# A two-layer decoder trunk on one core: the last K tile pair of the second two w2 blocks by seven products, and four sums of the first two blocks kept in PSUM

## The chip, the cores and the metric

The kernel runs on one core of a Trainium2 chip. Its time is the device time of one execution in microseconds (us); the median of several runs counts. The engines of the core work side by side and meet through semaphores: TensorE (PE in the profile; its weight loads are PEld) multiplies, VectorE (DVE) and ScalarE (ACT) do elementwise work, GpSimd (POOL) hardly anything here, and SyncE (SP) issues the DMA loads. TensorE writes its products into PSUM, which has eight banks of 128 x 512 float32.

## The reference, cut to what matters

Two layers over 256 tokens of width 2048: a short gated convolution mixer, then latent attention, each followed by the same MLP with 8192 hidden units. The change is in the MLP:

```
def sq_relu_mlp(x, w1, w2):
    return jnp.square(jax.nn.relu(x @ w1)) @ w2

h = layer_norm(ALPHA * h + mix, ln_g[layer, 0], ln_b[layer, 0])
h = layer_norm(ALPHA * h + sq_relu_mlp(h, mlp_w1[layer], mlp_w2[layer]),
               ln_g[layer, 1], ln_b[layer, 1])
```

x has 256 rows, w1 is 2048 x 8192, w2 is 8192 x 2048, all float32.

## The kernel before

**Split numbers.** Each float32 operand is kept as two parts: `hi`, the value rounded to fp32r, and `lo`, the rest. A product takes three matmuls, hi·hi, hi·lo and lo·hi (`dot`, L283 to L285). For weights the two parts are made on the core: a raw half unit of 128 x 1024 is loaded by SP (L132), ScalarE casts it to `hi` (L121), VectorE subtracts to get `lo` (L122). There are five raw buffers and eight pairs of `hi` and `lo`. `take` hands the next weights to TensorE and prepares further ones, as far as five half units ahead; a buffer's next load waits until its last reader is done.

**The MLP** (`mlp`, run as MLP 1 and MLP 3) goes through the 8192 hidden units in 8 passes of 1024, q = 0 to 7. A pass has a w1 stage, 8 products with w1 that give 8 hidden tiles (128 units x 256 tokens, collected by `hidden`), and a w2 stage, which multiplies these 8 tiles (the K tiles) with the pass's rows of w2 and adds to the accumulator `acc`: 2 token halves t by 4 column blocks n of 512.

**Plain blocks** (`down`): for each K tile and token half one `dot` of 128 x 512, so 8 x 2 x 3 = 48 matmuls per block; then `put` adds the block's two PSUM sums to `acc` on VectorE (L578).

**Seven products.** In the passes q = 1 to 6 (`FAST`) blocks 0 and 1 are done in another way (`first_pair`, `fast_products`): a pair of K tiles, two token halves and two column blocks make a 2 x 2 by 2 x 2 block product, and that is formed from seven products of sums instead of eight plain ones (`FACTORS` lists their names and factors). The sums of hidden tiles, S1 to S4, are made in `form` during the w1 stage. The sums of weights, T1 to T4, are made in `prepare` from two raw half units: beside three casts and three subtractions of 1024 columns, VectorE does L154 (1024 columns), L157, L160 and the low half of T4 (512 columns each). Such a unit counts as three in the look-ahead. Each of the seven products has a PSUM bank of its own and is summed there over the four K tile pairs of the pass. Then `keep` adds the seven sums to `acc` or to `sums` in SBUF (L588), seven additions per pass; those named "1", "5", "7" and "6" (`OWN`) go to `sums`. In the last pass `fold` (L607) adds `sums` into `acc` in six operations, beside the w1 stage.

**Banks.** `mlp` runs with all eight banks. The w1 stage turns between banks 0 and 1, the seven products use 2, 3, 4, 5, 6, 7 and 0 (`KEPT`), block 2 uses 1 and 2, block 3 uses 3 and 4. In the passes 1 to 4 of MLP 3 `extra` is `turn_residual`: four transposes for each token half into bank 5 or 6, and one addition on VectorE (L946).

**What sets the order.** Each engine runs its instructions in one fixed order. That order is made when the kernel is built: a scheduler places the instructions by priority and by its own estimate of when things become ready, so VectorE's queue interleaves the splitting of later weights with the collecting of sums. An instruction that waits holds up everything behind it on its engine.

One fast pass is therefore: w1 stage (256 matmuls, 512 and 256 columns in turn), four seven-product units (84 matmuls), block 2 and block 3 (96 matmuls).

Of the kernel before, what the change touches and what calls it, by code (L numbers as in the profile page):

```python
# [10 lines left out]
F32 = mybir.dt.float32  # L11
# [5 lines left out]
P = 128  # L17
# [17 lines left out]
NB = 4  # L35
BW = D // NB
FAST = range(1, NQ - 1)
FIRST = (0, 1, 2, 4, 6, 8, 12, 16)
HEAD = 4
GROUP = 3  # L40
# [10 lines left out]
def trunk(ctx: ExitStack, tc: tile.TileContext, xT, vecs, w_first, w_in, w_out, w_kv, w_q, w_uk, w_uv,  # L51
# [18 lines left out]
    def halves(w):  # L70

        lead = len(w.shape) - 2
        return [(w,)] if lead == 0 else [h for i in range(w.shape[0]) for h in halves(w[i])]
# [6 lines left out]
    def mlp_stream(l):  # L80
        out = []
        for q in range(NQ):
            out += halves(w1[l, q * QC:(q + 1) * QC])
            plain = halves(w2[l, q, 2:] if q in FAST else w2[l, q])
            fast = [(w2f[l, q, j, 0], w2f[l, q, j, 1]) for j in range(QC // 2)] if q in FAST else []
            at = 0 if q or q not in FAST else len(plain) // 2
            out += plain[:at] + fast + plain[at:]
        return out

    stream += mlp_stream(0) + halves(w_kv) + halves(w_q)  # L90
# [94 lines left out]
    def psum(name, bank=None):  # L185

        bank = Banks.next() if bank is None else bank
        return (pmm if bank < 4 else Banks.more).tile([P, 512], F32, tag=f"mm{bank}", name=name)
# [89 lines left out]
            yield ps  # L278


    def dot(ps, w, x, first, last):

        nc.tensor.matmul(ps, x[0], w[0], start=first, stop=False)  # L283
        nc.tensor.matmul(ps, x[0], w[1], start=False, stop=False)  # L284
        nc.tensor.matmul(ps, x[1], w[0], start=False, stop=last)  # L285

    def held(x, t):

        return [x[:, o + t * P:o + (t + 1) * P] for o in (0, T)]

    def wide_rows(w, kk):

        return [v[:, 4 * kk:4 * kk + 4, :].rearrange("p a c -> p (a c)") for v in w]

    def down(x, put, n, banks=(None, None), amid=None):

        ps = [psum("ps_d", bank) for bank in banks]
        for j in range(len(x) // 2):
            w, = take(1)
            for kk in range(2):  # L300
                k = 2 * j + kk
                for t in range(2):
                    dot(ps[t], wide_rows(w, kk), held(x[k], t), k == 0, k == len(x) - 1)
            if amid and 2 * j + 2 == len(x) // 2:
                amid()
        for t in range(2):
            put(n, t, ps[t])
# [10 lines left out]
                    dot(ps, wide_rows(ws[n, k // 2], k % 2), held(x[k], t), k == 0, k == len(x) - 1)  # L318
                put(n, t, ps)

    OWN, KEPT = ("1", "5", "7", "6"), (2, 3, 4, 5, 6, 7, 0)


    FACTORS = (("3", "S4", "22"), ("1", "11", "11"), ("5", "S1", "T1"), ("7", "S3", "T3"),
               ("2", "12", "21"), ("6", "S2", "T2"), ("4", "22", "T4"))

    def fast_products(ps, x, forms, j, n):

        b, = take(1)
        a = {"11": held(x[2 * j], 0), "12": held(x[2 * j + 1], 0), "22": held(x[2 * j + 1], 1)}  # L330
        for i in range(4):
            a[f"S{i + 1}"] = [forms[:, j, o, i * P:(i + 1) * P] for o in range(2)]
        for p, l, r in FACTORS:
            dot(ps[p], b[r], a[l], j == 0, j == n - 1)

    def whole(ps, out):

# [216 lines left out]
    def mlp(idx, ln, blocks, fast, begin=None, extra=None):  # L554
# [14 lines left out]
        def block(n, t):  # L569
            return acc[:, t, n * BW:(n + 1) * BW]  # L570
# [7 lines left out]
                nc.vector.tensor_tensor(block(n, t), block(n, t), ps, ALU.add)  # L578

        sums = fast.tile([P, 4, BW], F32, name=f"sums{idx}")  # L580

        def keep(p, ps):

            at = sums[:, OWN.index(p)] if p in OWN else block(*{"2": (0, 0), "3": (1, 0), "4": (0, 1)}[p])
            if q == 0 or q == FAST[0] and p in OWN:
                nc.scalar.copy(at, ps)
            else:
                nc.vector.tensor_tensor(at, at, ps, ALU.add)  # L588

        def first_pair(h, forms, banks):  # L590

            n = QC // 2
            ps = {p: psum(f"ps_f{p}", bank) for (p, _, _), bank in zip(FACTORS, banks)}
            for j in range(n):
                fast_products(ps, h, forms, j, n)
            for p in ps:
                keep(p, ps[p])

        def fold():

            s1, s5, s7, s6 = (sums[:, i] for i in range(4))
            both = acc[:, 1, :2 * BW].rearrange("p (b c) -> p b c", b=2)
            right = acc[:, :, BW:2 * BW]
            two = lambda v: v.unsqueeze(1).to_broadcast([P, 2, BW])
            for d, a, b in ((block(0, 0), block(0, 0), s1), (s6, s6, s1), (block(1, 0), block(1, 0), s6),
                            (s7, s7, s6), (both, both, two(s7)), (right, right, two(s5))):
                nc.vector.tensor_tensor(d, a, b, ALU.add)  # L607
                yield

        for q in range(NQ):  # L610
            ht = act.tile([P, QC, 2 * T], F32R, tag="c", name=f"h{idx}_{q}")
            h = [ht[:, k, :] for k in range(QC)]
            forms = None
            if q in FAST:
                forms = act.tile([P, QC // 2, 2, 4 * P], F32R, tag="a2", name=f"forms{idx}_{q}")
            pair = []

            def pair_tile(m):

                if m % 2 == 0:  # L620
                    pool = (act, "ab") if m % 4 else (fast, "fp")
                    t = pool[0].tile([P, 2 * T], F32, tag=pool[1], name="fp")
                    pair.append(t.rearrange("p (i t) -> p i t", i=2))
                return pair[-1]

            def form(j):
                (a11, a21), (a12, a22) = ((pair[j][:, i, :P], pair[j][:, i, P:]) for i in range(2))
                sf = fast.tile([P, 4, P], F32, tag="sf", name="sf")
                s1, s2, s3, s4 = (sf[:, i, :] for i in range(4))
                nc.vector.tensor_tensor(s1, a21, a22, ALU.add)  # L630
                nc.vector.tensor_tensor(s3, a21, a11, ALU.subtract)
                nc.vector.tensor_tensor(s2, s1, a11, ALU.subtract)
                nc.vector.tensor_tensor(s4, a12, s2, ALU.subtract)
                split(forms[:, j, 0, :], forms[:, j, 1, :], sf.rearrange("p i c -> p (i c)"))

            def hidden(m, ps, evac, *func):
                both = pair_tile(m) if q in FAST else None
                f = both[:, m % 2, :] if both is not None else tmp.tile([P, T], F32, tag="fh", name="fh", bufs=3)
                evac(ps, f, *func)
                if not func:  # L640
                    nc.scalar.activation(f, f, AF.Relu)  # L641
                nc.scalar.activation(f, f, AF.Square)
                if both is None:
                    put_split(h[m], f)
                elif m % 2:
                    at = ht[:, m - 1:m + 1, :]
                    split(at[:, :, :T], at[:, :, T:], both)
                    form(m // 2)

            if q == 0:  # L650
                for m in range(QC):
                    if m < GROUP:
                        if m == 0:
                            ws = ln.ws if ln.ws else group_of(GROUP)
                            if not ln.ws:
                                mm_wide(ws, ln.xd)
                            ln.finish()
                        ps = ws[m][1]
                    else:
                        ws = [(take(), psum("ps_w"))]  # L660
                        mm_wide(ws, ln.xd)
                        ps = ws[0][1]
                    hidden(m, ps, ln.weighted, AF.Relu)
                    if m > 0:
                        normal()
                if begin:
                    begin(range(1))
                acc = act.tile([P, 2, D], F32, tag="a1", name=f"acc{idx}")
            else:
                folds = fold()  # L670
                for m, ps in enumerate(products(QC, xhl, TURNED, (0, 1))):
                    hidden(m, ps, whole)
                    if q == NQ - 1:
                        next(folds, None)
                        if begin:
                            begin(range(max(2 * m, 1), 2 * m + 2))

            if q == NQ - 1:
                blocks(block, put, h)
                return  # L680
            if q == 0:
                for n in range(NB):
                    down(h, put, n)
            else:
                first_pair(h, forms, KEPT)
                for n, banks in ((2, (1, 2)), (3, (3, 4))):
                    down(h, put, n, banks)
                    if extra and n == 2 and q <= NB:
                        for t in range(2):
                            extra(block, q - 1, t, 5 + t)  # L690

    def to_wide(block, put, h):

# [406 lines left out]
```

## Time and profile before

| | us |
|---|---|
| median of 3 runs | 2025.86 (2025.52 to 2026.03) |
| the profiled execution | 2028.49 |
| its span, first to last instruction | 2026.4 |
| VectorE, low half of a raw half unit (L122), 710 times | 1.222 each |
| ScalarE, cast of a raw half unit (L121), 710 times | 1.051 each |
| VectorE, addition of a plain block's sum (L578), 64 times | 0.681 each |
| VectorE, additions of seven-product sums (L588), 76 times | 0.681 each |
| w loads of 512 KB (`in_w_dram`), 416 times, issue to landing | 4.3, the median |
| w2f loads of 512 KB (`in_w2f_dram`), 96 times | 3.6, the median |

The durations of one instruction contain a tail that overlaps the next one on the same engine, so that a row of them advances faster than the sum of durations. Records of matmuls overlap as well; the distance between two starts is what a matmul costs.

### The profile page before, as it was taken

How to read it: one execution, taken by the hardware profiler on the slowest of the kernel's cores; microseconds unless marked ns; L12 is line 12 of the kernel's file. 1: busy time of each engine (PE TensorE's matmuls, PEld its weight loads, DVE VectorE, ACT ScalarE, POOL GpSimd, SP SyncE). 2: the span in 40 equal slices, each digit the busy share in tenths (PEclk: the TensorE clock that was granted, in tenths of full speed). 3: DMA queues.
4: the chain of work that ended last, by engine and by line, in shares of the span. 5: the costliest groups of instructions: out<-in, count | busy, mean ns of one | idle time of the engine just before them, and what ended most of it. 6: DMA issues, size and time to landing. Idle time of an engine off the chain costs nothing.

```text
span 2026.4 us, 30052 instructions
## 1 busy us (share of the span) xinstructions
PE 2018.3 (100%) x11240; PEld 1763.1 (87%) x11240; DVE 1605.8 (79%) x2467; ACT 1176.2 (58%) x1797; POOL 2.3 (0%) x21
## 2 busy tenths in 40 slices
PE   9999999999999999999999999999999999999998
PEld 8888888988888888888889998898888888888886
DVE  7667667787787978979678978776879798797966
ACT  6444445576565665656556655566656566565651
POOL 0000000000000000000000000000000000000000
PEclk9999999999999999999999999999999999999999
DMA  8666666564746657475654543656475664746663
GB/s 298 204 188 189 190 187 186 177 196 146 249 148 226 204 170 239 143 240 194 220 179 146 179 134 126 197 177 196 137 249 167 198 227 142 248 160 210 220 201 120
DMA packets 106849, 385.30 MB, mean 190 GB/s; under 512 B 11856, under 2 KB 12752, under 8 KB 106448
## 3 DMA queue, kind: packets, MB, share of 16 engines
q1 hardware_dynamic: 106560, 383.27, 59.3%
q8 instruction: 88, 1.44, 0.3%
q14 instruction: 57, 0.47, 0.1%
q10 hardware_dynamic: 144, 0.13, 0.0%
HBM read 381.25 MB, written 2.10 MB: 189 GB/s over the span
## 4 chain that ended last, share of the span: by engine, by line
PE 99%; DMA 0%; DVE 0%; SPq 0%; issue 0%; ACT 0%; DVEq 0%
PE ps_u L199 20%; PE ps_l L199 13%; PE ps_u L203 11%; PE ps_d L285 7%; PE ps_d L283 7%; PE ps_d L284 7%; PE ps_l L203 7%; PE ps_f L284 4%; PE ps_f L285 4%; PE ps_f L283 4%; PE ps_w L233 2%; PE ps_w L231 2%; PE ps_w L232 2%; PE ps_g L231 1%; PE ps_g L233 1%; PE ps_g L232 1%
## 5 line engine op out<-in xcount | busy, mean ns | idle before, releaser
L122 DVE TENSOR_TENSOR lo<-raw,hi 128x1024 fp32r<-128x1024 f32 x710 | 859.8, 1222 | 314.1 <-ACT hi L121 243.0
L121 ACT CAST hi<-raw 128x1024 fp32r<-128x1024 f32 x710 | 742.4, 1051 | 460.0 <-PE ps_u L199 108.0
L199 PE MATMUL ps_u<-xhl,hi 128*128 128x512 f32 x1792 | 621.0, 391 | 0.0
L203 PE MATMUL ps_u<-xhl,lo 128*128 128x256 f32 x1792 | 499.5, 280 | 0.0
L199 PEld LDWEIGHTS ps_u<-xhl,hi 128*128 128x128 f32 x1792 | 334.2, 187 | 72.4
L203 PEld LDWEIGHTS ps_u<-xhl,lo 128*128 128x128 f32 x1792 | 338.6, 189 | 1.8
L283 PE MATMUL ps_d<-hi,h 128*128 128x512 f32 x640 | 249.8, 390 | 0.0
L285 PE MATMUL ps_d<-hi,h 128*128 128x512 f32 x640 | 249.1, 389 | 0.0
L284 PE MATMUL ps_d<-lo,h 128*128 128x512 f32 x640 | 249.0, 389 | 0.0
L199 PE MATMUL ps_l<-xhl_a,hi 128*128 128x512 f32 x704 | 243.5, 392 | 0.0
L203 PE MATMUL ps_l<-xhl_a,lo 128*128 128x256 f32 x704 | 194.8, 279 | 0.0
L199 PEld LDWEIGHTS ps_l<-xhl_a,hi 128*128 128x128 f32 x704 | 131.7, 187 | 29.5
L283 PEld LDWEIGHTS ps_d<-hi,h 128*128 128x128 f32 x640 | 120.2, 188 | 25.0 <-DVE fh L340 0.3
L285 PEld LDWEIGHTS ps_d<-hi,h 128*128 128x128 f32 x640 | 120.1, 188 | 24.9
L284 PEld LDWEIGHTS ps_d<-lo,h 128*128 128x128 f32 x640 | 120.2, 188 | 24.7
L203 PEld LDWEIGHTS ps_l<-xhl_a,lo 128*128 128x128 f32 x704 | 132.2, 188 | 0.2
L199 PE MATMUL ps_l<-z,hi 128*128 128x512 f32 x240 | 83.9, 398 | 0.0
L641 ACT ACTIVATE fp<-fp 128x256 f32<-128x256 f32 x96 | 40.0, 416 | 72.6 <-DVE fp L340 71.9
L121 ACT CAST hi_t<-raw_t 128x1024 fp32r<-128x1024 f32 x48 | 50.4, 1050 | 42.9 <-DVE raw_t L154 33.4
L233 PE MATMUL ps_w<-xd,hi 128*128 128x258 f32 x256 | 73.0, 285 | 0.0
L231 PE MATMUL ps_w<-xd,hi 128*128 128x258 f32 x256 | 72.6, 284 | 0.0
L232 PE MATMUL ps_w<-xd,lo 128*128 128x258 f32 x256 | 72.4, 283 | 0.0
(257 smaller groups left out, 3134.5 us busy)
## 6 DMA issues: line engine op xcount, KB each, us to landing
raw<-in_w_dram SPq DMA_DIRECT2D x416, 512.0 KB, 4.3
raw<-in_w2f_dram SPq DMA_DIRECT2D x96, 512.0 KB, 3.6
raw<-in_w_in_dram SPq DMA_DIRECT2D x88, 512.0 KB, 3.6
raw<-in_w_out_dram SPq DMA_DIRECT2D x32, 512.0 KB, 3.9
raw<-in_w_o_dram SPq DMA_DIRECT2D x32, 512.0 KB, 4.3
raw<-in_w_kv_dram SPq DMA_DIRECT2D x10, 512.0 KB, 4.2
raw<-in_w_q_dram SPq DMA_DIRECT2D x8, 512.0 KB, 4.5
raw<-in_w_uk_dram SPq DMA_DIRECT2D x8, 512.0 KB, 4.4
```

The costliest lines, as they stand in the source:

```text
L121: nc.scalar.copy(hi, src)
L122: nc.vector.tensor_tensor(lo, src, hi.bitcast(F32), ALU.subtract)
L199: nc.tensor.matmul(ps, w[blk // 8][0][:, blk % 8, :], x, start=first, stop=False)
L203: nc.tensor.matmul(ps[:, :T], w[blk // 8][1][:, blk % 8, :], x[:, :T], start=False, stop=last)
L231: nc.tensor.matmul(ps[:, :W], hi, x[k][:, :W], start=k == 0, stop=False)
L232: nc.tensor.matmul(ps[:, :W], lo, x[k][:, :W], start=False, stop=False)
L233: nc.tensor.matmul(ps[:, :W], hi, x[k][:, W:], start=False, stop=k == NC - 1)
L283: nc.tensor.matmul(ps, x[0], w[0], start=first, stop=False)
L284: nc.tensor.matmul(ps, x[0], w[1], start=False, stop=False)
L285: nc.tensor.matmul(ps, x[1], w[0], start=False, stop=last)
L641: nc.scalar.activation(f, f, AF.Relu)
```

## The change

In the fast passes, blocks 2 and 3 are no longer plain over all eight K tiles. Block 3 and then block 2 are done plainly over the first six, and the last pair of K tiles (`SECOND`) goes through seven products for both blocks together. These seven are not summed in PSUM: each is finished on its own and collected at once, into `acc` or into `sums`. They go round the banks c, b, d, a, c, b, d.

The four sums "1", "5", "7" and "6" of blocks 0 and 1 now stay in banks 4 to 7 from the first fast pass to the last, summed over all six passes, and `fold` reads them there. Only the sums "3", "2" and "4" of these blocks are collected in each pass. `sums` in SBUF now holds the four of blocks 2 and 3, and `fold` has twelve operations and a copy, two operations per hidden tile. All else in the MLP's fast passes has the four banks 0 to 3, in roles a, b, c, d that change from pass to pass (`turn`). One matmul of a plain block, the middle one of the first `dot` of block 2, is done as two of 256 columns. The residual's transposes come after the first pair of K tiles of block 3 and of block 2, one token half each. The host lays out w2 for both pairs of blocks.

```diff
@@ mlp_stream
-            plain = halves(w2[l, q, 2:] if q in FAST else w2[l, q])
-            fast = [(w2f[l, q, j, 0], w2f[l, q, j, 1]) for j in range(QC // 2)] if q in FAST else []
-            at = 0 if q or q not in FAST else len(plain) // 2
-            out += plain[:at] + fast + plain[at:]
+            if q not in FAST:
+                out += halves(w2[l, q])
+                continue
+            out += [(w2f[l, q, 0, j, 0], w2f[l, q, 0, j, 1]) for j in range(QC // 2)]
+            for n in (3, 2):
+                out += halves(w2[l, q, n, :SECOND])
+            out.append((w2f[l, q, 1, SECOND, 0], w2f[l, q, 1, SECOND, 1]))
@@ dot
-    def dot(ps, w, x, first, last):
+    def dot(ps, w, x, first, last, two=False):
...
-        nc.tensor.matmul(ps, x[0], w[1], start=False, stop=False)
+        for at in (slice(0, T), slice(T, 2 * T)) if two else (slice(None),):
+            nc.tensor.matmul(ps[:, at], x[0], w[1][:, at], start=False, stop=False)
@@ down
-            if amid and 2 * j + 2 == len(x) // 2:
+            if amid and j == 0:
@@ mlp
+        own = {}
+
+        def gather(at, ps, first=False):
+            if first:
                 nc.scalar.copy(at, ps)
             else:
                 nc.vector.tensor_tensor(at, at, ps, ALU.add)
 
+        def alone(p, g):
+
+            return block(*{"2": (2 * g, 0), "3": (2 * g + 1, 0), "4": (2 * g, 1)}[p])
+
         def first_pair(h, forms, banks):
 
             n = QC // 2
-            ps = {p: psum(f"ps_f{p}", bank) for (p, _, _), bank in zip(FACTORS, banks)}
+            ps = {p: psum(f"ps_f{p}", bank) for p, bank in zip("324", banks)}
+            if q == FAST[0]:
+                own.update({p: psum(f"ps_o{p}", 4 + i) for i, p in enumerate(OWN)})
             for j in range(n):
-                fast_products(ps, h, forms, j, n)
-            for p in ps:
-                keep(p, ps[p])
+                def put_product(p, w, x):
+                    if p in OWN:
+                        dot(own[p], w, x, q == FAST[0] and j == 0, q == FAST[-1] and j == n - 1)
+                    else:
+                        dot(ps[p], w, x, j == 0, j == n - 1)
+
+                fast_products(h, forms, j, put_product)
+            for p in "324":
+                gather(alone(p, 0), ps[p])
+
+        def second_pair(h, forms, banks):
+
+            c, b, d, a = banks
+            for n, two, free, split_at in ((3, (b, c), a, None), (2, (d, a), b, (0, 0))):
+                def amid():
+                    if extra and q <= NB:
+                        extra(block, q - 1, 3 - n, free)
+
+                down(h[:2 * SECOND], put, n, two, amid, split_at)
+            places = iter((c, b, d, a, c, b, d))
+
+            def put_product(p, w, x):
+                ps = psum(f"ps_s{p}", next(places))
+                dot(ps, w, x, True, True)
+                if p in OWN:
+                    gather(sums[:, OWN.index(p)], ps, q == FAST[0])
+                else:
+                    gather(alone(p, 1), ps)
+
+            fast_products(h, forms, SECOND, put_product)
 
         def fold():
...
+            t = raws.tile([P, 1024], F32, tag="raw", name=f"fold{idx}")
+            nc.scalar.copy(t[:, :BW], own["1"])
+            for g in range(2):
+                s1, s5, s7, s6 = (own[p] if g == 0 else sums[:, i] for i, p in enumerate(OWN))
...
+        turn = 0, 1, 2, 3
...
-                first_pair(h, forms, KEPT)
-                for n, banks in ((2, (1, 2)), (3, (3, 4))):
-                    down(h, put, n, banks)
-                    if extra and n == 2 and q <= NB:
-                        for t in range(2):
-                            extra(block, q - 1, t, 5 + t)
+                a, b, c, d = turn
+                first_pair(h, forms, (c, d, a))
+                second_pair(h, forms, (c, b, d, a))
+                turn = a, c, b, d
```

More of the change, by code (lines that the diff above doesn't have):

```diff
@@ L37 @@
 FAST = range(1, NQ - 1)
+SECOND = QC // 2 - 1
 FIRST = (0, 1, 2, 4, 6, 8, 12, 16)
@@ L293, in wide_rows, with down @@
         return [v[:, 4 * kk:4 * kk + 4, :].rearrange("p a c -> p (a c)") for v in w]
-    def down(x, put, n, banks=(None, None), amid=None):
+    def down(x, put, n, banks=(None, None), amid=None, two=None):
         ps = [psum("ps_d", bank) for bank in banks]
@@ L302, in down @@
                 for t in range(2):
-                    dot(ps[t], wide_rows(w, kk), held(x[k], t), k == 0, k == len(x) - 1)
-            if amid and 2 * j + 2 == len(x) // 2:
+                    dot(ps[t], wide_rows(w, kk), held(x[k], t), k == 0, k == len(x) - 1, (k, t) == two)
+            if amid and j == 0:
                 amid()
@@ L319, in down_late, with fast_products @@
                 put(n, t, ps)
-    OWN, KEPT = ("1", "5", "7", "6"), (2, 3, 4, 5, 6, 7, 0)
+    OWN = ("1", "5", "7", "6")
     FACTORS = (("3", "S4", "22"), ("1", "11", "11"), ("5", "S1", "T1"), ("7", "S3", "T3"),
                ("2", "12", "21"), ("6", "S2", "T2"), ("4", "22", "T4"))
-    def fast_products(ps, x, forms, j, n):
+    def fast_products(x, forms, j, put):
         b, = take(1)
@@ L333, in fast_products @@
         for p, l, r in FACTORS:
-            dot(ps[p], b[r], a[l], j == 0, j == n - 1)
+            put(p, b[r], a[l])
     def whole(ps, out):
@@ L580, in mlp @@
         sums = fast.tile([P, 4, BW], F32, name=f"sums{idx}")
-        def keep(p, ps):
-            at = sums[:, OWN.index(p)] if p in OWN else block(*{"2": (0, 0), "3": (1, 0), "4": (0, 1)}[p])
-            if q == 0 or q == FAST[0] and p in OWN:
+        own = {}
+        def gather(at, ps, first=False):
+            if first:
                 nc.scalar.copy(at, ps)
@@ L599, in fold @@
         def fold():
-            s1, s5, s7, s6 = (sums[:, i] for i in range(4))
-            both = acc[:, 1, :2 * BW].rearrange("p (b c) -> p b c", b=2)
-            right = acc[:, :, BW:2 * BW]
             two = lambda v: v.unsqueeze(1).to_broadcast([P, 2, BW])
[L605 to L608, printed above, removed]
+            t = raws.tile([P, 1024], F32, tag="raw", name=f"fold{idx}")
@@ new lines, in fold @@
+            nc.scalar.copy(t[:, :BW], own["1"])
+            for g in range(2):
+                s1, s5, s7, s6 = (own[p] if g == 0 else sums[:, i] for i, p in enumerate(OWN))
+                u1, u = (t[:, :BW], t[:, BW:]) if g == 0 else (s1, s6)
+                both = acc[:, 1, 2 * g * BW:(2 * g + 2) * BW].rearrange("p (b c) -> p b c", b=2)
+                right = acc[:, :, (2 * g + 1) * BW:(2 * g + 2) * BW]
+                for d, x, y in ((block(2 * g, 0), block(2 * g, 0), u1), (u, u1, s6),
+                                (block(2 * g + 1, 0), block(2 * g + 1, 0), u), (u, u, s7), (both, both, two(u)),
+                                (right, right, two(s5))):
+                    nc.vector.tensor_tensor(d, x, y, ALU.add)
+                    yield
@@ L669, in mlp @@
             else:
-                folds = fold()
-                for m, ps in enumerate(products(QC, xhl, TURNED, (0, 1))):
+                folds = fold() if q == NQ - 1 else iter(())
+                for m, ps in enumerate(products(QC, xhl, TURNED, turn[:2])):
                     hidden(m, ps, whole)
+                    for _ in range(2):
+                        next(folds, None)
                     if q == NQ - 1:
-                        next(folds, None)
                         if begin:
@@ L1079 @@
         "w2": np.stack([np.stack([_rows(q) for q in w.reshape(NQ, QC * P, D)]) for w in a["mlp_w2"]]),
-        "w2f": np.stack([np.stack([_pairs(q[:, :2 * BW]) for q in w.reshape(NQ, QC * P, D)]) for w in a["mlp_w2"]]),
+        "w2f": np.stack([np.stack([np.stack([_pairs(q[:, 2 * g * BW:2 * (g + 1) * BW]) for g in range(2)])
+                                   for q in w.reshape(NQ, QC * P, D)]) for w in a["mlp_w2"]]),
         "cosT": np.tile(cos, (4, 1)),
```

## The prediction

> **What bounds the kernel now.** I read the head of the page first, then the stages of one pass, then VectorE and ScalarE around the place of the change.
>
> ```profile
> span 2026.4 us, 30052 instructions
> PE 2018.3 (100%) x11240; PEld 1763.1 (87%) x11240; DVE 1605.8 (79%) x2467; ACT 1176.2 (58%) x1797; POOL 2.3 (0%) x21
> ...
> PE 99%; DMA 0%; DVE 0%; SPq 0%; issue 0%; ACT 0%; DVEq 0%
> ```
>
> TensorE never rests, and it is 99% of the chain that ended last: a matmul taken away is time won, and any wait given to TensorE is time lost. The busy time by stage of one fast pass (MLP 1; columns: window, length, then busy us of PE, PEld, DVE, ACT, POOL):
>
> ```profile
> 628.54:672.93 44.39, 44.39 (x257) 39.12 (x256) 35.26 (x52) 27.57 (x45) 0.00 (x0) 1.00 0.55 171
> 672.93:692.01 19.08, 19.08 (x86) 15.78 (x85) 17.53 (x25) 12.26 (x16) 0.00 (x0) 1.00 0.54 162
> 692.01:713.77 21.76, 21.76 (x97) 18.02 (x96) 18.88 (x21) 11.59 (x11) 0.00 (x0) 1.00 0.84 314
> ```
>
> These are the w1 stage, the four seven-product units of blocks 0 and 1, and the plain blocks 2 and 3. VectorE is idle 9.1 us in the first, 1.5 in the second, 2.9 in the third: 13.5 of 85.2 us. Its average of 79% hides that the third stage, where the change falls, has almost nothing free. Here is VectorE there in another pass, whose plain stage begins at 777.25 us, then ScalarE's casts of the raw weights (last column: idle time before, and what ended it):
>
> ```profile
> 777.24 1.23 DVE L122 TENSOR_TENSOR lo<-raw,hi 128x1024 fp32r<-128x1024 f32 x1 [1.60 <-ACT hi L121]
> ...
> 780.12 1.27 DVE L588 TENSOR_TENSOR sums<-sums,ps_f 128x512 f32<-128x512 f32 x2
> ...
> 783.10 5.76 DVE L122 TENSOR_TENSOR lo<-raw,hi 128x1024 fp32r<-128x1024 f32 x5
> ```
>
> ```profile
> 788.10 1.06 ACT L121 CAST hi<-raw 128x1024 fp32r<-128x1024 f32 x1 [2.34 <-DMA raw<-in_w_dram]
> 790.54 1.06 ACT L121 CAST hi<-raw 128x1024 fp32r<-128x1024 f32 x1 [1.38 <-DMA raw<-in_w_dram]
> ```
>
> Five 1024-column subtractions in 5.76 us are 1.14 us each; two 512-column additions in 1.27 us are 0.60 each plus the last one's tail of 0.08. The casts wait for DMA: the issues at 784.35 and 785.48 (SP's rows) landed when these casts began, 3.75 and 5.06 us later. So a raw buffer that is freed late is a weight that comes late. TensorE shows no wait, because eight banks let every sum be collected late.
>
> **The change, part by part.**
>
> *Matmuls removed.* Per fast pass blocks 2 and 3 lose 24 of 96 matmuls and gain 21. The 96 take 21.76 us (606.78 to 628.54), 0.227 each. 12 passes x 3 x 0.227 = **-8.2 us**.
>
> *One matmul split in two halves.* Matmuls of 256 columns follow each other at 0.12 us (ps_k, 1115.6 on); two for one of 0.227 is 0.01 x 12 = +0.2 us.
>
> *VectorE per pass.* One seven-product unit replaces two plain half units: four 1024-column operations and three of 512 (4 x 1.14 + 3 x 0.60 = 6.4) for two of 1024 (2.3): +4.1. Sums to collect: 3 + 4 + 7 = 14 for 11: +1.8. So +5.9 against 13.5 idle: as an average it fits. It does not fit where it stands, and there are now four rotating banks instead of eight.
>
> *The order.* The order of the changed program's instructions is the same in every pass, but for what the first one leaves to ScalarE and the residual's additions (both below). VectorE does, from the beginning of the plain stage: low half of the 4th plain unit (a), collect, 5th, collect, 6th, the unit for the seven products (low, T, two differences, low of T), collect block 3 twice, low of its second tile (b), low of T4, four w1 halves (c1 to c4), **collect block 2 twice, collect product 3, one more w1 half, collect 1, 5, 7, 2, 6, 4**. TensorE's product 5 waits for block 2's first addition (same bank), 7 for the second, 2 for product 3 collected, 6 for 1, 4 for 5. SP issues c3's raw load when T's low half is done, c4's when (b) is done.
>
> With t = 0 at the first matmul of the plain stage, TensorE without waits ends block 3 at 8.16 (36 x 0.227), block 2 at 16.32, the seven products (21) at 21.08. VectorE begins (a) between -0.95 and +1.43 in the twelve passes, at -0.2 in the mean; in today's order the same work stands in front of it. From there, with 1.14 and 0.60, and 0.1 more for each dependent pair:
>
> ```
> VectorE: a, collect, 5th, collect, 6th        -0.2 .. 4.4
> unit's low, T, two differences, low of T       4.4 .. 9.2   -> c3's load issued 9.3
> collect block 3 twice (ready 8.4)              9.2 .. 10.4
> b, T4, c1, c2                                 10.4 .. 14.5  -> c4's load issued 11.7
> c3 (landed 13.6, cast 14.7)                   14.7 .. 15.8
> c4 (landed 16.0, cast 17.05)                  17.1 .. 18.2
> collect block 2 twice                         18.2 .. 19.4
> collect 3, w1 half, collect 1, 5              19.4 .. 22.4
> TensorE: 3, 1 at 16.32 .. 17.68; 5 waits 1.25 to 18.9; 7, 2 to 21.0; 6 waits 0.9 to 21.9; 6, 4 to 23.25
> ```
>
> The landing is the step that I choose: 4.3 us, the median of the 416 w loads in the page's part 6. Its bounds are 3.4 (the least of the whole trace) and 5.1 (the second of a burst, above). ScalarE's cast is 1.05. The seven products end 2.2 us late; minus 0.68 saved, a pass loses **1.5 us**. In the first fast pass of each MLP ScalarE copies 1, 5, 7, 6, so that VectorE's collecting doesn't hold 6: only the first wait, 1.25 - 0.68 = 0.6 us lost. Sum: 10 x 1.5 + 2 x 0.6 + 0.2 = **+16 us**. With 3.4: 10 x 0.6 - 2 x 0.3 = +6. With 5.1: 10 x 2.3 + 2 x 1.4 = +26.
>
> What follows is not late: a w1 stage begins with four halves ready (11.1 us of TensorE) and VectorE's backlog (4 additions, 3 halves, 5.8 us) goes into the stage's 9.1 us.
>
> *At nothing:* six more operations of fold and a ScalarE copy in each last pass (4 x 0.60 + 2 x 1.14 = 4.7 us, VectorE; 0.6, ScalarE), hidden in a w1 stage where VectorE is busy 26.5 of 44.4; uncovered, 9.4 us for both MLPs. The raw buffer that fold holds leaves four; a load, cast and low half take 4.3 + 1.05 + 1.14 = 6.5 us, over four 1.6, under the 2.8 in which TensorE uses a half unit; uncovered, with the trace's longest landing of 11.6, (11.6 + 2.2) / 4 = 3.5, so 0.7 us more for some five halves of each MLP. Bytes and loads stay. In four passes of MLP 3 two residual additions of 0.60 move into this row, against 0.9 us of transposes on TensorE, in the passes before already: nothing either way, within 0.5 us each.
>
> **The rivals.**
>
> *The clock falls too.* At the opening TensorE waits 1.86 us (8.33 to 10.20), and the granted clock (third column from the right) answers:
>
> ```profile
> 9.00:11.00 2.00, 0.80 (x3) 0.67 (x4) 1.51 (x4) 1.39 (x6) 0.00 (x0) 1.00 1.04 416
> 11.00:13.00 2.00, 2.00 (x9) 1.66 (x8) 1.99 (x6) 1.88 (x7) 0.00 (x0) 0.69 1.04 424
> 13.00:15.00 2.00, 2.00 (x9) 1.89 (x9) 2.00 (x6) 1.91 (x7) 0.00 (x0) 0.50 1.06 442
> 15.00:17.00 2.00, 2.00 (x12) 1.65 (x11) 1.63 (x3) 0.96 (x1) 0.00 (x0) 0.96 0.99 404
> ```
>
> That loses 2 x 0.31 + 2 x 0.50 + 2 x 0.04 = 1.7 us. My two waits of 1.25 and 0.9 us lie within 4.2 us. If every pass paid this, +20 more: 2062; if half of them, 2052. Against it: at 2018.5 TensorE waits 1.2 us and the clock in the next 2.8 us reads 1.00. The Trainium skill (TensorE: Matmul & The Clock Gate, "A second HAM failure mode: psum-queue depth-cycling") describes just this: a kernel that goes round PSUM banks idles briefly between groups and its clock swings to half and back; the same page (Part 1) lets a window of about 3.4 us decide. By that page the sum would be the 2062 above, by the gap at 2018.5 the 2042 below; the opening agrees with the page in the fall to 0.50.
>
> *The waits are about as long as what is saved.* With loads at 3.4 us and (a) at -0.95, the earliest pass of today, the waits are 0.5 us, and passes come out even: 2022 to 2030.
>
> *The bank waits vanish and only the matmuls count.* If (c3) and (c4) are ready as early as TensorE needs their successors, block 2's additions stand at 16.5, product 5 waits for nothing, and all of the 8.2 us is won: 2018. It needs (b) some 2.2 us earlier than the ledger; for it, four additions have left the beginning of the stage (2.4 us, in the ledger already) and SP has fewer loads in flight. From an average wait under 0.68 us on the change wins. That the change does less than it says is excluded: the changed program has 11085 matmuls for 11109, that is -36 + 12.
>
> **How the numbers follow.** The profiled execution took 2028.5 us for a span of 2026.4; the median of the runs shown is 2025.86. The sum +16 makes 2044.5 of the former and **2042** of the median. Chances: ledger 0.60 (2031 to 2052), clock 0.17 (2052 to 2062), even 0.13 (2022 to 2030), won 0.10 (2018). The range 2024 to 2060 leaves out the last and the top of the clock's, under 2 in 10. A measurement of this kernel tells 0.2% (4 us) from no change: faster 0.10, same 0.12, slower 0.78.
>
> **What would show it.** PE waits that appear only in the seven-product groups of blocks 2 and 3, ended by VectorE's additions, first before product 5 (1.25 us), then before 6 (0.9); none before 5 would make the third rival right. ScalarE's cast of c4 ended by DMA, at about t = 16. PEclk staying 1.00 excludes the clock. From one pass to the next 85.24 - 0.7 + 2.2 = 86.7 us. Wrong would be waits in the w1 or first-pair stages: then the load on VectorE as such is the bound, not this order.

## The result and the profile after

The changed kernel takes 2050.39 us (median of 4 runs, 2049.29 to 2051.84), the kernel before 2025.94 on the same chip (4 runs): a ratio of 1.0119, 95% interval 1.0106 to 1.0132, so **24.5 us slower**. The head of the page of the changed kernel, and its chain of work by engine:

```profile
span 2048.6 us, 30210 instructions
...
PE 2019.5 (99%) x11216; PEld 1754.8 (86%) x11216; DVE 1681.9 (82%) x2575; ACT 1192.4 (58%) x1823; POOL 2.3 (0%) x21
...
PE 80%; DVE 12%; DMA 5%; issue 3%; ACT 1%; SPq 0%; ACTq 0%; DVEq 0%
```

TensorE was 99% of the chain and is 80% of it now; VectorE and the DMA have come in. The head hides this: the busy share of TensorE only goes from 100% to 99%, because a few waits of 1 to 2 us are little beside 2048. What TensorE waits for (columns: waiting tile and line, releaser, total us, times, longest):

```profile
PE ps_s L287 <- DVE acc L583: 12.7, 9, 2.1
PE ps_s L287 <- DVE sums L592: 4.8, 9, 0.6
PE turned L987 <- DVE acc L592: 3.6, 4, 1.6
```

ps_s are the seven products of blocks 2 and 3. The first row is product 5, waiting for block 2's addition to empty its bank; the second is product 6, waiting for product 1 to be collected; the third is the residual's transposes in MLP 3. Before the change none of these rows existed.

By stages, in the two profiled executions: every w1 stage (44.39 us) and every four units of blocks 0 and 1 (19.08) is as long as before within 0.02, but for two w1 stages of 45.20. The stage of blocks 2 and 3 grew from 21.76 us (22.66 with transposes) to 22.89 to 25.09. Its twelve excesses add up to 22.2 us, which is the whole difference of the spans (2048.6 - 2026.4). The w1 stages' +1.6 is made up for by the opening, where TensorE waited 1.6 us instead of 1.9 and its clock did not fall.

VectorE in one such stage, which begins at 783.87 us (add that to the prediction's ledger to compare; columns: start, us, engine, line, operation, idle before and what ended it):

```profile
783.78 1.22 DVE L126 TENSOR_TENSOR lo<-raw,hi 128x1024 fp32r<-128x1024 f32 x1 [1.41 <-ACT hi L125]
...
792.11 1.22 DVE L126 TENSOR_TENSOR lo_t<-raw_t,hi_t 128x1024 fp32r<-128x1024 f32 x1
793.25 1.28 DVE L583 TENSOR_TENSOR acc<-acc,ps_d 128x512 f32<-128x512 f32 x2
794.45 1.22 DVE L126 TENSOR_TENSOR lo<-raw,hi 128x1024 fp32r<-128x1024 f32 x1
795.58 0.68 DVE L126 TENSOR_TENSOR t<-raw,t 128x512 fp32r<-128x512 f32 x1
796.18 3.48 DVE L126 TENSOR_TENSOR lo<-raw,hi 128x1024 fp32r<-128x1024 f32 x3
801.00 1.23 DVE L126 TENSOR_TENSOR lo<-raw,hi 128x1024 fp32r<-128x1024 f32 x1 [1.33 <-ACT hi L125]
802.14 1.28 DVE L583 TENSOR_TENSOR acc<-acc,ps_d 128x512 f32<-128x512 f32 x2
803.34 0.68 DVE L592 TENSOR_TENSOR acc<-acc,ps_s 128x512 f32<-128x512 f32 x1
803.94 1.22 DVE L126 TENSOR_TENSOR lo<-raw,hi 128x1024 fp32r<-128x1024 f32 x1
805.07 1.87 DVE L592 TENSOR_TENSOR sums<-sums,ps_s 128x512 f32<-128x512 f32 x3
```

ScalarE's casts of the raw halves c3 and c4 in the same stage:

```profile
796.97 1.05 ACT L125 CAST hi<-raw 128x1024 fp32r<-128x1024 f32 x1 [1.69 <-DMA raw<-in_w_dram]
799.92 1.05 ACT L125 CAST hi<-raw 128x1024 fp32r<-128x1024 f32 x1 [1.90 <-DMA raw<-in_w_dram]
```

And TensorE, from the last matmul of product 1 on:

```profile
801.36 0.39 PE L290 MATMUL ps_s<-hi,h 128*128 128x512 f32 x1
802.97 0.47 PE L287 MATMUL ps_s<-hi_t,forms 128*128 128x512 f32 x1 [1.23 <-DVE acc L583]
803.28 0.39 PE L289 MATMUL ps_s<-lo_t,forms 128*128 128x512 f32 x1
...
804.87 0.39 PE L290 MATMUL ps_s<-hi,h 128*128 128x512 f32 x1
805.81 0.50 PE L287 MATMUL ps_s<-hi,forms 128*128 128x512 f32 x1 [0.55 <-DVE sums L592]
806.15 0.40 PE L289 MATMUL ps_s<-lo,forms 128*128 128x512 f32 x1
```

Block 2's last matmul starts at 800.00. Its two additions could begin at about 799.8 and 800.4 (experiment 7 shows them 15.9 and 16.6 us into the stage); VectorE stands idle 1.33 us at that time, but next in its queue is the low half of c4 (801.00), which waits for a cast that waits for a load. So block 2 is collected from 802.14 on, and product 5 needs that bank. **A load for a later stage, which has nothing to do with the bank, holds TensorE.** Of the 2.4 us that the collecting is late, 1.3 are this idle time and 1.1 the low half itself. In eleven of the twelve stages the cast of c4 waits last for its load, in one for TensorE.

### The profile page after: what moved, and what is told of

Its sections match the earlier page's. It is cut to its first block, busy times and chain, and to the rows that moved or that the text cites. A ratio compares the mean times of both kernels' runs of the same rounds, so it can differ in the third digit from the quotient of the medians.

```text
span 2048.6 us, 30210 instructions
## 1 busy us (share of the span) xinstructions
PE 2019.5 (99%) x11216; PEld 1754.8 (86%) x11216; DVE 1681.9 (82%) x2575; ACT 1192.4 (58%) x1823; POOL 2.3 (0%) x21
## 4 chain that ended last, share of the span: by engine, by line
PE 80%; DVE 12%; DMA 5%; issue 3%; ACT 1%; SPq 0%; ACTq 0%; DVEq 0%
PE ps_u L203 20%; PE ps_l L203 13%; PE ps_u L207 10%; PE ps_l L207 7%; DMA raw<-in_w_dram 4%; DVE lo L126 4%; PE ps_d L287 3%; PE ps_d L290 3%; PE ps_d L289 3%; DVE lo_t L126 2%; PE ps_w L237 2%; PE ps_w L235 2%; PE ps_w L236 2%; DVE raw_t L158 1%; ACT hi L125 1%
## 5 line engine op out<-in xcount | busy, mean ns | idle before, releaser
L287 PE MATMUL ps_d<-hi,h 128*128 128x512 f32 x544 | 213.1, 392 | 0.0
L290 PE MATMUL ps_d<-hi,h 128*128 128x512 f32 x544 | 212.0, 390 | 0.0
L289 PE MATMUL ps_d<-lo,h 128*128 128x512 f32 (+1 forms) x556 | 211.8, 385 | 0.0
L289 PEld LDWEIGHTS ps_d<-lo,h 128*128 128x128 f32 x556 | 104.4, 188 | 21.4
L290 PEld LDWEIGHTS ps_d<-hi,h 128*128 128x128 f32 x544 | 102.1, 188 | 21.1
L287 PEld LDWEIGHTS ps_d<-hi,h 128*128 128x128 f32 x544 | 102.2, 188 | 20.6 <-DVE fh L345 0.3
L125 ACT CAST hi_t<-raw_t 128x1024 fp32r<-128x1024 f32 x60 | 63.1, 1051 | 77.8 <-DVE raw_t L158 66.4
L158 DVE TENSOR_TENSOR raw_t<-raw,raw 128x1024 f32<-128x1024 f32 x60 | 73.0, 1217 | 6.6 <-DMA raw<-in_w2f_dram 6.5
L126 DVE TENSOR_TENSOR lo_t<-raw_t,hi_t 128x1024 fp32r<-128x1024 f32 x60 | 73.2, 1220 | 1.5
L237 PE MATMUL ps_w<-xd,hi 128*128 128x258 f32 x256 | 72.9, 285 | 0.0
```

Source lines behind the costliest of these rows:

```text
L125: nc.scalar.copy(hi, src)
L126: nc.vector.tensor_tensor(lo, src, hi.bitcast(F32), ALU.subtract)
L158: nc.vector.tensor_tensor(t.rearrange(two, a=2), b12.unsqueeze(1).to_broadcast([P, 2, BW]), r1.rearrange(two, a=2), ALU.subtract)
L237: nc.tensor.matmul(ps[:, :W], hi, x[k][:, W:], start=False, stop=k == NC - 1)
L289: nc.tensor.matmul(ps[:, at], x[0], w[1][:, at], start=False, stop=False)
```

## The experiments

The theory: TensorE's waits come from the order of VectorE's queue in this one stage, where the halves c3 and c4 stand ahead of block 2's sums. Rivals: VectorE simply has too much to do; or the four sums in PSUM cost time by themselves; or the split matmul, or the transposes, do.

**1. Sums first.** The seven products' unit prepares nothing ahead when it is taken, and the following w1 halves are put behind the last collected product in VectorE's queue. The same instructions in another order:

```diff
@@ split
-        nc.vector.tensor_tensor(lo, src, hi.bitcast(F32), ALU.subtract)
+        low = nc.vector.tensor_tensor(lo, src, hi.bitcast(F32), ALU.subtract)
+        if state.get("behind") is not None:
+            tc.add_manual_dep(low.ins, state["behind"].name, ...)
@@ products
+            state["behind"] = state.pop("after", None)
             w = take()
+            state["behind"] = None
@@ second_pair
-            fast_products(h, forms, SECOND, put_product)
+            fast_products(h, forms, SECOND, put_product, 0)
+            state["after"] = last[0].ins
```

> The changed kernel with another order on VectorE: the low halves of the five w1 half units that follow the seven products of blocks 2 and 3 are queued behind the last of the seven additions, instead of two of them before block 2's additions and one between the additions of products 3 and 1. Theory (the bank waits come from the order of VectorE's queue and from the late load in front of block 2's additions): block 2 is collected from t = 16.5 to 17.7, the waits before products 5 and 6 go, the matmuls saved count, and only the waits of the residual's transposes (3.6 us in all) stay: 2026 - 8 + 4 = 2022, between 2018 and 2024. Rival (VectorE's 5.9 us more work per pass is the bound, wherever it stands): the work is the same, so 2045 to 2055, with the waits moved into the w1 stage.

Measured: 2025.25 us (10 runs), ratio 0.9996 (0.9986 to 1.0005) to the kernel before: 25 us below the changed kernel, no difference from before. Both waits of the products are gone, but for 0.6 us in one first pass (there for a copy by ScalarE); in MLP 1 the other five stages are 21.11 us, 93 matmuls at 0.227. It ended 1 us above the range that the theory gave. The largest wait that is left to TensorE, at the transposes, has grown from 3.6 us:

```profile
PE turned L994 <- DVE acc L597: 5.4, 4, 2.1
```

The transposes at the beginning of block 3 need a bank whose sum VectorE collects only 3.5 to 5.0 us into the stage. The four stages that have them take 22.90, 26.01, 23.53 and 23.72 us instead of 22.66; the longest holds a fall of the clock too.

**2. Two more additions in front of block 2's.** They write into a spare tile; 24 of 0.60 in all, 14.4 us of VectorE:

```diff
@@ down
+        if two:
+            for t in range(2):
+                two_more(ps[t])
         for t in range(2):
             put(n, t, ps[t])
+
+    def two_more(ps):
+        nc.vector.tensor_tensor(state["spare"], state["spare"], ps, ALU.add)
```

> The changed kernel with two more additions of 512 columns on VectorE per fast pass (0.60 each; they read block 2's sums into a spare tile that nothing uses), each queued before one of block 2's two additions. Theory (order and banks): all that follows on VectorE comes 1.2 us later and TensorE waits for it, in twelve passes +14 us: about 2064, between 2058 and 2068. Rival (work as such): 1.2 us go into the 9 us that VectorE has free in each w1 stage, so 2050 to 2053.

Measured: 2067.86 us, ratio 1.021 (1.0188 to 1.0232), 17.5 above the changed kernel: the added 14.4 us reached TensorE in full, and more (the mean granted clock of the profiled execution is 0.997 for 0.999). The waits grew where the additions stand:

```profile
PE ps_s L287 <- DVE acc L589: 18.8, 20, 2.4
PE ps_s L287 <- DVE acc L600: 7.5, 9, 0.9
```

**3. Ten more additions in the kernel before.** Is it VectorE's load as such? The kernel before, with ten more 512-column additions into a spare tile in every fast pass, three for each token half of block 2 and two for each of block 3, in front of the real one:

```diff
@@ down (before)
         for t in range(2):
+            for _ in range((3, 2)[n - 2] if banks[0] is not None else 0):
+                nc.vector.tensor_tensor(state["spare"], state["spare"], ps[t], ALU.add)
             put(n, t, ps[t])
```

> The kernel before with the work that the change adds on VectorE, and nothing else: in each fast pass ten more additions of 512 columns (0.60 each, 6.0 us; from the plain blocks' sums into a spare tile that nothing uses), queued before the additions of blocks 2 and 3. Theory (it isn't the work, it is that a bank is needed again at once): with eight banks nothing waits for these additions, and what is late goes into the next w1 stage's 9 us: 2026 to 2029. Rival (work in this stage as such: 18.9 + 6.0 = 24.9 us in a stage of 21.76): 12 x 3.1, about 2063.

Measured: 2026.40 us, ratio 0.9998 (0.9989 to 1.0008): nothing. Its plain stage of MLP 1 (columns: window, length, busy us of PE, PEld, DVE, ACT, POOL):

```profile
689.83:711.59 21.76, 21.76 (x98) 18.02 (x96) 20.61 (x25) 12.32 (x12) 0.00 (x0) 1.00 0.83 307
```

VectorE is busy 1673.6 us in this kernel, nearly as long as in the changed one (1681.9), and 20.61 of the 21.76 us here, and TensorE waits in none of the twelve stages. There the load is not the bound. With eight banks a sum may be collected late; with four in rotation, and products that need one again at once, it may not (experiment 2).

**4. The sums in PSUM alone.** Blocks 2 and 3 are plain over all eight K tiles again; the four sums still stay in banks 4 to 7 and all else has four banks:

```diff
@@ mlp_stream
-                out += halves(w2[l, q, n, :SECOND])
-            out.append((w2f[l, q, 1, SECOND, 0], w2f[l, q, 1, SECOND, 1]))
+                out += halves(w2[l, q, n])
@@ second_pair
-                down(h[:2 * SECOND], put, n, two, amid, split_at)
...
+                down(h, put, n, two, amid)
...
@@ mlp
-                turn = a, c, b, d
+                turn = b, c, d, a
```

> One part of the change alone: the four sums of blocks 0 and 1 stay in PSUM over the passes, the rest has four banks, but blocks 2 and 3 are plain over all eight K tiles (the banks' roles turn so that the w1 stage begins with block 3's). No matmul is saved, VectorE has four additions less per pass than the kernel before. Theory (the loss comes from seven products that each need a bank again within 2.7 us): 2026, between 2023 and 2030. Rival (four banks instead of eight are the cost by themselves): some 1.5 us per pass, 2040 or more.

Measured: 2033.97 us, ratio 1.0035 (1.0023 to 1.0047): 4 us above the theory's range, and below the rival's. Its eight stages without transposes are 21.76 us, as before; the four with them 26.88, 24.07, 23.83 and 24.37 instead of 22.66, 8.5 us more. So the transposes seem to cost it, and the sums nothing by themselves. The only new wait:

```profile
PE turned L975 <- DVE acc L591: 5.9, 4, 2.5
```

**5. The same, with block 3's transposes one half unit later** (at 5.4 us of the stage instead of 2.7):

```diff
@@ down
-            if amid and j == 0:
+            if amid and j == (n == 3):
```

> The kernel with the four sums in PSUM and plain blocks 2 and 3 (2034.0 us in its earlier run), block 3's transposes one half unit later. Theory (its whole loss against the kernel before is TensorE's wait at the transposes: stages of 26.88, 24.07, 23.83 and 24.37 us for 22.66 are 8.5 us): 2024 to 2028, the time of the kernel before. Rival (part of it is the sums in PSUM by themselves): 2030 or more.

Measured: 2026.78 us, ratio 1.0002 (0.9993 to 1.0011). The four stages are 22.70 to 22.73 us. That settles it: this half of the change is free if the transposes come after their bank is collected.

**6. The changed kernel with the transposes later**, the same one line and nothing else.

> The changed kernel with block 3's transposes one half unit later and nothing else. Theory (the wait at the transposes and the wait before product 5 are two places of one delay: what TensorE waits at the first it does not wait at the second, since block 2's additions stand in the same queue at a time of their own): the transposes' 3.6 us of waits go, the waits before product 5 of those four passes rise from 0, 0, 0 and 0.4 to 1 to 2 us each; 2048 to 2052, no change against the 2050.4 of the changed kernel. Rival (they are separate costs): 2046 to 2047.

Measured: 2051.60 us, ratio 1.0124 (1.011 to 1.0137), against 1.0119 for the changed kernel: no gain. The row of the transposes is gone, and the first row rose from 12.7 us in 9 waits to 17.0 in 12:

```profile
PE ps_s L287 <- DVE acc L583: 17.0, 12, 2.4
```

What TensorE no longer waits at the transposes it waits before product 5, since block 2's addition still comes when c4 has come: in the four stages with transposes the waits there rise from 0.55 us to 3.37 together (by 0.2 to 1.1 each, less than expected), and these stages take 96.8 us together for 97.0. The rest of the row's rise lies in the other stages. Two rows in a table of waits may be one delay, paid where TensorE meets it first.

**7. Both: sums first, and the transposes later.** Edits 1 and 5 together.

> The changed kernel with VectorE's queue put in order (sums first, as in the earlier run that gave 2025.3 us) and block 3's transposes of the residual one half unit later, at 5.4 us of the stage in place of 2.7. Theory (all that was left there of the expected gain is TensorE's wait at these transposes, 0.59 + 2.13 + 1.22 + 1.47 = 5.4 us, for the bank whose sum is collected only at 3.5 to 5.0 us of the stage): the wait goes, the four passes take 22.0 us each, 2025.3 - 5.4 = 2019.9, and 1.7 less where no clock fall is in it: 2017 to 2021, faster than the kernel before. Rival (the delay moves on: the residual's additions stand behind the unit's differences and hold the bank of a later product): 2024 to 2028, with waits named after products in place of the transposes.

Measured: **2021.42 us** (9 runs, 2019.46 to 2023.98), ratio 0.9978 (0.9968 to 0.9987): 5.0 us faster than the kernel before, 29 faster than the change as it was made, a few tenths above the theory's range. The head of its page:

```profile
span 2018.8 us, 30165 instructions
...
PE 2010.6 (100%) x11216; PEld 1754.7 (87%) x11216; DVE 1687.4 (84%) x2575; ACT 1191.9 (59%) x1823; POOL 2.3 (0%) x21
```

VectorE's busy share is higher than in the changed kernel (84% for 82%, with the same instructions), and the kernel is faster. The same stage as above, now from 773.93 us on:

```profile
784.42 1.22 DVE L126 TENSOR_TENSOR lo<-raw,hi 128x1024 fp32r<-128x1024 f32 x1
785.55 0.68 DVE L126 TENSOR_TENSOR t<-raw,t 128x512 fp32r<-128x512 f32 x1
786.16 2.35 DVE L126 TENSOR_TENSOR lo<-raw,hi 128x1024 fp32r<-128x1024 f32 x2
789.81 1.37 DVE L589 TENSOR_TENSOR acc<-acc,ps_d 128x512 f32<-128x512 f32 x2 [1.30 <-PE ps_d L296]
791.17 0.69 DVE L597 TENSOR_TENSOR acc<-acc,ps_s 128x512 f32<-128x512 f32 x1
```

VectorE's idle time of 1.3 us is still there, but it now waits for TensorE and not for a load: block 2 is collected at t = 15.9 instead of 18.3. The eight stages without transposes are 21.11 us but for one first pass (22.22), the four with them 22.06 to 22.66. Together they are 5.1 us shorter than before, of the 8.2 that the matmuls are worth; the rest is 1.1 us in that first pass (0.46 of it a wait for a copy by ScalarE), 1.7 in the stages with transposes (0.4 of it waits for the residual's addition), and 0.03 in each stage, 0.65 for 0.68.

**8. The split matmul done whole.**

```diff
@@ second_pair
-            for n, two, free, split_at in ((3, (b, c), a, None), (2, (d, a), b, (0, 0))):
+            for n, two, free, split_at in ((3, (b, c), a, None), (2, (d, a), b, None)):
```

> The changed kernel without the one matmul in two halves of 256 columns (a matmul of 512 as elsewhere). The theory and the ledger give it 0.01 us per pass: 2050, within 2 us. Rival (the split shifts the order or the weight loads to a gain): 5 us or more slower without it.

Measured: 2049.34 us, ratio 1.0107 (1.009 to 1.0124): no difference from the change.

**9. Six raw buffers.** With one more buffer c4's load need not wait for (b). To make room, two small tiles that only set addresses were taken out, so a control has those out and keeps five buffers (all but the first pair of lines):

```diff
-RAW, WA = 5, 8
+RAW, WA = 6, 8
...
-    for tag, columns in (("c", 4096), ("pad0", 64), ("b", 8256), ("a1", 4128), ("pad1", 96), ("a2", 4128), ("pad2", 96)):
+    for tag, columns in (("c", 4096), ("pad0", 64), ("b", 8256), ("a1", 4128), ("a2", 4128), ("pad2", 96)):
         act.tile([P, columns], F32, tag=tag, name=f"at_{tag}")
-    small.tile([P, 32], F32, tag="pad", name="at_pad", bufs=1)
```

> The changed kernel with six raw buffers instead of five (room for it from two unused padding tiles). Theory: the raw load of the fourth w1 half unit is issued some 2.3 us earlier, so that nothing on VectorE waits for a load before block 2's additions; the wait before product 5 goes, that before product 6 (0.5 to 0.9) and the transposes' stay: 2018 + 6 + 4 = 2028, between 2023 and 2034. Rival (work as such): the work is the same, 2045 to 2055. Rival (order alone, the load doesn't matter): about 2045.

> A control for the run with six raw buffers: the changed kernel with five raw buffers, without the same two padding tiles, so that other tiles lie at other addresses. Every theory: the changed kernel's time, 2050, within 3 us.

Measured: 2068.88 us, ratio 1.0208 (1.0192 to 1.0223) with six buffers; 2056.80, ratio 1.0156 (1.0139 to 1.0173) for the control. Both misses. What TensorE waits for with six:

```profile
PE ps_d L286 <- DVE acc L591: 20.1, 12, 4.0
...
PE ps_s L286 <- DVE acc L591: 0.7, 2, 0.3
```

The waits of the products vanished but for 0.7 us, and not for the expected reason. With other buffers the scheduler makes another order: the first pair's three sums now stand behind one more low half, and block 3, which needs their banks, waits 0.7 to 4.0 us at the beginning of each stage. TensorE is therefore late already when it comes to the products. Block 2 is collected 17.4 to 22.4 us into the stage, on the average no earlier than in the changed kernel (17.7 to 19.9), and VectorE still stands idle 0.7 to 1.0 us before c4's low half in ten of the twelve stages. The cast of c4 is now held by TensorE, in all twelve, and no longer by its load; here in the stage that begins at 608.75:

```profile
624.22 1.05 ACT L124 CAST hi<-raw 128x1024 fp32r<-128x1024 f32 x1 [1.75 <-PE ps_d L289]
```

So another resource than the raw buffer bound the preparing, probably one of the eight pairs that TensorE still reads (not tested), and what an earlier load alone would do to block 2's sums is open. The control shows the second part (columns as above; its w1 and first-pair stages, which take 44.39 and 19.08 us in the changed kernel):

```profile
543.77:588.71 44.94, 44.94 (x257) 39.37 (x256) 36.14 (x53) 27.74 (x46) 0.00 (x0) 1.00 0.54 171
588.71:608.14 19.43, 19.43 (x86) 15.81 (x85) 18.18 (x25) 12.71 (x17) 0.00 (x0) 1.00 0.55 167
```

With those two tiles gone each of these stages is 1 to 2% longer, at full clock and without a wait: 12 x (0.55 + 0.35) = 10.8 us. Its waits before products 5 and 6 are shorter in return, 7.0 us together for 17.5. Which of the two tiles does it, and what it changes about the addresses, was not tried.

## Why the prediction was right, and where it was not

The forecast was 2042 (2024 to 2060) and slower; the time was 2050.39. The mechanism held, step by step.

*The matmuls removed* (-8.2 us) are real: 21.11 us for 21.76 wherever nothing waits (experiments 1 and 7). *The halves* cost nothing that can be measured (8). *VectorE's average* is not the bound (3), as the sum of 5.9 against 13.5 said; no wait appeared in the w1 and first-pair stages.

*The ledger*, in the stage shown: (a) at -0.1 (chosen -0.2); block 3 collected at 9.4 (9.2); c3's load issued at 9.5 (9.3) and landed within 3.6 us, c4's issued at 11.8 (11.7) and landed within 4.2 (chosen: 4.3); c4's low half at 17.1 (17.1); block 2 collected at 18.3 (18.2); the seven products end at 23.46 (23.25). The landing, the step marked as a choice, was right for c4, on which block 2's sums wait; c3's was 0.7 us shorter than chosen, which changed nothing, because VectorE was busy until 14.6.

*The two waits.* Predicted 1.25 and 0.9, as time lost by TensorE. The rows say 1.23 and 0.55, but a row counts idle time after a modelled end of 0.39. By starts the first costs 802.97 - 801.36 - 0.227 = 1.38, and 0.08 more because the next matmul follows after 0.31 instead of 0.227: 1.47. The second costs 0.71 + 0.11 = 0.83. So both were sized about right, and 1.47 + 0.83 - 0.68 = 1.6 us is what 23.46 has over 21.76, within 0.1.

*The term that was mis-sized* is (a)'s start: chosen at -0.2, the mean of the kernel before. In the changed kernel it starts between -1.0 and +0.8, at 0.2 in the mean, 0.4 later. The loads hardly vary: block 2's addition follows the low half of T4 by 6.5 to 7.0 us in eleven of twelve stages (6.7 in the ledger), whether that is early (11.2) or late (13.2). So the waits before product 5, 0.69 to 2.15 us where no transposes stand, were inherited from the beginning of the stage, and 12 x 0.4 = 5 us went into the sum. With the fall of the clock in one stage, below, 1.7, that is about the 6 us between the +16 of the forecast and the stages' +22.2. The control of experiment 9 points the same way: there (a) starts at -0.4 in the mean, and the waits before products 5 and 6 are 7.0 us in all for 17.5. Why (a) starts later in the changed kernel was not tested. The rest, to the medians' 24.5, is that the profiled execution of before was itself 2.6 us over its median.

*First passes*: 0.6 us each was predicted, 1.38 and 0.56 came. *Fold and the raw buffer it holds*, priced at nothing: the w1 stages beside fold are 44.40 and 44.39 us, so right. *The transposes*, "nothing either way, within 0.5 us each", were wrong as a place and right as a sum: TensorE waits 0.6 to 1.6 us there, because block 3's transposes moved ahead of the collecting of the bank they use, but in the changed kernel the wait before product 5 shrinks by as much (6). The step would have failed as soon as the larger delay went: 5.4 us of waits in experiment 1, 8.5 us of stage in experiment 4.

*The clock rival* came true in one stage of twelve (columns: window, length, busy us by engine, then the granted clock):

```profile
626.00:629.00 3.00, 2.44 (x6) 2.00 (x7) 3.00 (x5) 1.04 (x1) 0.00 (x0) 0.59 1.02 404
629.00:632.00 3.00, 3.00 (x13) 2.43 (x12) 2.98 (x6) 1.86 (x2) 0.00 (x0) 0.84 0.65 208
```

3 x 0.41 + 3 x 0.16 = 1.7 us, after a wait of 2.10 us: the price was right, the number of times was not the twelve that the rival needed. *The rival that all is won* named the point on which everything turns, block 2's additions no later than their matmuls. Experiments 1 and 7 put them there by order rather than by an earlier (b), and the waits were gone.

## What to carry to other kernels

Before a change takes PSUM banks away or lets them turn faster, write down the fixed order of the engine that collects them, and ask of each collecting instruction what stands in front of it and what that waits for: here two halves for a later stage, the second still on its way from memory, turned a saving of 8 us into a loss of 24. Put the collecting ahead of work for later stages, and check whether that only moves the wait to the next place that uses the same banks. A busy share says nothing about either: in the best kernel here VectorE has the highest one, 84%.

## What was not expected of the hardware

*When the clock falls.* After waits of 1.6 to 2.7 us TensorE's granted clock sometimes fell and sometimes did not, and length alone does not decide. In the kernel without the halves (columns as above), the stage around 801 has a wait of 2.27 us, that around 977 one of 2.43:

```profile
801.30:806.10 4.80, 3.79 (x15) 2.80 (x16) 4.80 (x8) 2.57 (x3) 0.00 (x0) 1.00 0.91 329
...
977.20:982.60 5.40, 5.05 (x15) 4.05 (x16) 5.39 (x9) 2.53 (x3) 0.00 (x0) 0.68 0.67 218
```

In the changed kernel 2.10 us brought a fall and 2.07 and 2.15 none; with the transposes later 1.88, 2.07 and 2.36 brought one and 1.97 none. The extremes are a fall about a microsecond after a wait of 1.64 us (experiment 2, around 804) and none after one of 2.74 us (experiment 9 with six buffers, around 874). The Trainium skill (TensorE: Matmul & The Clock Gate, Part 1) has a window of some 3.4 us that runs freely and does not start anew with the kernel, which would make it a matter of where in the window a wait falls. The rows agree with that in that a longer wait may pass unpunished; the window's own place is in no trace here. The swinging that the page describes for kernels that go round PSUM banks ("A second HAM failure mode: psum-queue depth-cycling") shows as single falls: one in twelve stages here, three in twelve with the transposes later.

*Matmuls can be slower at full clock.* Beside the 1 to 2% of the tiles taken out, two w1 stages of the changed kernel took 45.20 us for 44.39 with a granted clock of 1.00 throughout; the traces do not show why.
